# First feed-forward of a two-layer encoder: store issue, order of products, activation sums and conditioning work rearranged

## The chip, the cores and the metric

One core of a Trainium2 chip runs the whole program in one launch. The metric is the device time of that launch in microseconds (us), from three runs: a median of 2532.66, between 2530.72 and 2534.92.

## The reference

Input `x` is 1024 tokens by 1024 channels in float32; `c` is one conditioning vector of 1024. Two layers run one after the other. Each sub-layer computes `x <- LayerNorm(alpha*x + gate(c) * f(x*(1+scale(c)) + shift(c)))`.

```python
for l in range(2):
    sh1, sc1, g1, sh2, sc2, g2 = split(silu(c) @ w_ada[l] + b_ada[l], 6)
    h = x * (1 + sc1) + sh1
    if l == 0: y = short_conv_mixer(h)                  # W_out(B * conv3(C * V))
    else:      y = forgetting_attention(h, k, v, F)     # k, v, F from x after layer 0, own shift/scale
    x = layer_norm(alpha * x + g1 * y)
    h = x * (1 + sc2) + sh2
    y = (silu(h @ w_gate) * (h @ w_up)) @ w_down        # 1024 -> 2816 -> 1024
    x = layer_norm(alpha * x + g2 * y)
```

## The kernel before

The order of the work is: the convolution mixer of layer 0, the first feed-forward (layer 0), the shared K, V and forget gates with the queries (`kvq`), attention, and the second feed-forward. The activations lie channel-major: tile `x[k, half]` holds 128 channels by 512 tokens. Every matrix product in float32 is three matmuls (`mm3`, lines 169 to 171): each operand is split in a rounded part hi and a rest lo, and hi*hi, hi*lo and lo*hi are summed in PSUM. The split of a 128x1024 weight page is one ScalarE cast (line 655) and one VectorE subtraction (line 656) in `split_f`.

The first feed-forward is done by a Strassen-Winograd scheme: each matrix is cut in 2x2 blocks and seven block products M1 to M7 take the place of eight. `hidden` makes gate and up for 11 pairs of 128-channel tiles of the 2816 hidden channels; `down` then does the contraction. In `hidden` the work is a written list of **slots**, one product (j, n) each, pair j, n of M1 to M7. A slot is 24 matmuls of 128x512. There are 77: M1 and M2 of the six early pairs make the first 12, which are woven with the steps of the preceding LayerNorm for the second half of the tokens; then 65 slots run in a plain loop. An early pair has M5, M6, M3, M7 and, behind the next pair's first product, M4 there. A later pair has M1, M5, M6, M2, M3, M7 and its M4.

Each slot i does this in program order, and every engine keeps that order:

- `lq_pump(FRUN)`: issues loads from the written queue `lq` while more than FRUN pages are free. A page is 128x1024 float32; all loads, splits and results of this stage come from one first-in first-out list of free pages. The queue holds weight blocks (line 667, two DMAs for gate and up), the spilled M1 sums (815), stored blocks (822), and in each of the 65 slots one quarter of a conditioning group (755). All of them are issued on SP, the queue of SyncE.
- `ahead(i)`: the split of slot i+2, and on GpSimd the sums of weight blocks for slot i+3 (858 to 863, in place).
- the two halves of the product; behind each half its result leaves PSUM (`evac`): kept by ScalarE (895), summed with M1 on VectorE (900), or finished in `out` (913 silu input, 914 silu, 930 up part on VectorE, 931 product on GpSimd). `derive` (939, GpSimd) makes the sums of results that the contraction needs, and `store` (809) issues each to DRAM on SP as soon as it is written in the program. SP waits there until the data are ready.
- `ada_slot`: two VectorE multiply-adds (260, 262) on one quarter (two tiles of 128x512) of a conditioning group. A group is four quarters; when the next begins, four small TensorE transposes (295) and a VectorE reduction (297) finish it. What is left of the list is done in a loop behind the last slot.

The steps of the LayerNorm (`ln_steps`) are woven beside the 12 first slots. Each of the last four, `scale(k)` for k of 4 to 7, also runs the whole of `sums(k-4)` (lines 688 to 714): activation sums for M5, M6, M4, M7 and M3, two affine maps of x on GpSimd, and the store of two x tiles (738, SP).

`kvq` makes V (`values`) and K (`proj`) with 24 matmuls an item, and one `W.pump` now and then issues weights on SP.

Of the kernel before, what the change touches and what calls it, by code (L numbers as in the profile page):

```python
# [14 lines left out]
P = 128  # L15
# [62 lines left out]
class Builder:  # L78
# [369 lines left out]
    def ln_steps(self, half, tail, keep=False):  # L448
# [50 lines left out]
        return ([mean] + [lambda k=k: center(k) for k in range(KD)] + [var] + [lambda: None] * 2 + [spread]  # L499
                + [lambda k=k: scale(k) for k in range(KD)])  # L500
# [150 lines left out]
    def split_f(self, src, n=1024):  # L651

        nc = self.nc
        hi, lo = self.fpage((P, 1024), F32R), self.fpage((P, 1024), F32R)
        nc.scalar.copy(hi[:, 0:n], src)  # L655
        nc.vector.tensor_tensor(lo[:, 0:n], src, hi[:, 0:n], op=ALU.subtract)  # L656
        return hi, lo

# [13 lines left out]
    def sums_tail(self, vecs):  # L672
# [15 lines left out]
        def sums(k):  # L688
            K = k + 4
            a, a2 = A[:, k:k + 1], A[:, K:K + 1]  # L690
            z11, z12, z21, z22 = self.x[k, 0], self.x[k, 1], self.x[K, 0], self.x[K, 1]
            t = self.t("tmp", [P, HALF], tag="tA", bufs=3)
            u = self.t("tmp", [P, HALF], tag="tB", bufs=3)
            v = self.t("tmp", [P, HALF], tag="tA", bufs=3)
            w = self.t("tmp", [P, HALF], tag="tB", bufs=3)
            nc.gpsimd.tensor_scalar(t, z11, a, 1.0, op0=ALU.mult, op1=ALU.mult)
            nc.vector.scalar_tensor_tensor(u, z12, a, t, op0=ALU.mult, op1=ALU.subtract)
            put("M5", k, u, None, None)
            nc.vector.scalar_tensor_tensor(v, z22, a2, u, op0=ALU.mult, op1=ALU.subtract)
            put("M6", k, v, None, B[:, K:K + 1])  # L700
            nc.vector.scalar_tensor_tensor(w, z21, a2, v, op0=ALU.mult, op1=ALU.subtract)
            put("M4", k, w, None, None)
            nc.gpsimd.tensor_tensor(t, v, t, op=ALU.subtract)
            put("M7", k, t, None, BD[:, k:k + 1])
            h = self.T["M3"][k] = self.fpage((P, 2, HALF), F32R)
# [7 lines left out]
            self.x_out(k, K)  # L713
            self.sums_left -= 1

        def tail(k, half):
            if half == 0:
                n = "M1" if k < 4 else "M2"
                store = {}
                if (k, 0) in self.h:  # L720
                    self.drop("h", self.h.pop((k, 0)))
                self.modulate_tile(k, 0, self.x[k, 0], A, B, t_act=k % 2 == 0, lo_pool=k % 2 == 1, store=store)
                self.T[n][k % 4] = store[k, 0]
            elif k >= 4:
                sums(k - 4)
# [33 lines left out]
    def ada_slot(self):  # L759

        if not self.adal:
            return
        j, a = self.adal.pop(0)
        if a == 0:
            if self.adap:
                self.ada_finish(*self.adap)
            self.adap = None
            self.gacc = self.t("ada", [P, HALF], tag="ga", bufs=1)
        if a is None:
            return  # L770
        w = self.lq_get(("ada", j, a))
        for i in range(2):
            self.ada_step(self.gacc, w[:, i], 2 * a + i, self.nc.vector)
        self.lq_drop(("ada", j, a))
        if a == 3:
            self.adap = j, 4, self.gacc

    def hidden(self, l, nearly, left):
# [8 lines left out]
        nfirst = len(slots)  # L787
        late = None
        for j in range(npairs):
            names = ["M5", "M6", "M3", "M7"] if j in early else ["M1", "M5", "M6", "M2", "M3", "M7"]  # L790
# [16 lines left out]

        def store(n, j, t):
            nc.sync.dma_start(self.dr[n][j * P:(j + 1) * P], t)
            self.stored.add((n, j))  # L810
# [17 lines left out]
        def queue(lo, hi, ada):  # L828

            for i in range(lo, hi):  # L830
# [13 lines left out]
                if i >= nfirst and ada:  # L844
                    self.lq.append(ada.pop(0))
            self.lq += ada
# [18 lines left out]
        def parts(i):  # L865
# [3 lines left out]
            pre[i] = self.split_f(self.lq_get(key).rearrange("p m k c -> p (m k c)"))  # L869
            if e or n in end:  # L870
                self.lq_drop(key)

        def product(i, m):
# [13 lines left out]
            if m == 1:  # L887
                self.drop("f", *pre.pop(i))
# [13 lines left out]
        def leave(s, *names):  # L902
            for n in names:
                self.drop("f", s.pop(n))

        def out(j, r, half, s, m, bank, other):
# [16 lines left out]
            elif left and (r, half) == (0, 1):  # L923
                y = s["ya"][:, 1]
            else:
# [31 lines left out]
        def evac(i, m):  # L957
# [4 lines left out]
            if n == "M1":  # L962
                keep(s, "m1", m, X)
                if e and m:
                    nc.sync.dma_start(self.dr["m1"][j * P:(j + 1) * P], s["m1"].rearrange("p a b -> p (a b)"))
                    leave(s, "m1")
# [40 lines left out]
        def steps(i):  # L1007
            out = [lambda: ahead(i)]
# [4 lines left out]
            return out  # L1013
# [7 lines left out]
        def run(beside, before_end):  # L1021
            queue(2, len(slots), self.adaq_lq())
# [3 lines left out]
            for i in range(nfirst, len(slots)):  # L1026
                self.lq_pump(FRUN)
# [4 lines left out]
                self.ada_slot()  # L1032
            while self.adal:
                self.ada_slot()
            if self.adap:
                self.ada_finish(*self.adap)
                self.adap = None
        return begin, run

    def adaq_lq(self):  # L1040

        if self.adap:
            self.ada_finish(*self.adap)
            self.adap = None
        self.adal = [(j, a) for j in self.adaq for a in range(4)]
        self.adaq = []
# [50 lines left out]
    def down(self, update):  # L1097
# [37 lines left out]
        def part(ci, n, own, gi):  # L1135
# [7 lines left out]
            s = pg[:, 0:w].rearrange("p a b -> p (a b)")  # L1143
            if w == 2:
                pre[ci, n, own, gi] = self.split_f(s), None
            else:
                h = self.fpage((P, 2, HALF), F32R)
                nc.scalar.copy(h[:, 0], s)
                nc.vector.tensor_tensor(h[:, 1], s, h[:, 0], op=ALU.subtract)
                pre[ci, n, own, gi] = (h[:, 0], h[:, 1]), h  # L1150
            if not own or (key and n in ("M7", "M4", "M5", "M3")):
                self.lq_drop(key)
# [906 lines left out]
```

## Time and profile before

| | |
|---|---|
| median of 3 runs | 2532.66 us |
| profiled execution, its own time | 2534.88 us |
| its span (first to last instruction) | 2533.1 us |
| TensorE (PE) busy | 2396.6 us, 95% |
| VectorE (DVE) busy | 1508.8 us, 60% |
| GpSimd (POOL) busy | 854.6 us, 34% |
| ScalarE (ACT) busy | 825.4 us, 33% |
| mean granted TensorE clock | 0.98 |

All times in the rows count from the start of the span. A wait is listed as who waited for whom, with total us, number of times and longest. "SPq" is the queue of SyncE that issues DMAs. Matmul records can be missing by a few per cent, and the busy share of PE does not show how densely matmuls follow each other; their number in a stretch does.

### The profile page before, as it was taken

What the parts mean: (1) busy time and instruction counts of PE and PEld (TensorE: products, weight loads), DVE (VectorE), ACT (ScalarE), POOL (GpSimd) and SP (SyncE); (2) the same over time, 40 slices, a digit from 0 to 9 for tenths busy, and PEclk for the clock granted to TensorE, in tenths of its full rate; (3) what the DMA queues carried; (4) which work ended last, traced back from release to release, by engine and by line L of the source; (5) the groups of instructions that cost most, each with busy time, mean ns of one, the idle gap of its engine ahead of it and who ended that gap; (6) DMA issues with size and microseconds to landing.
All of it is one profiled execution on the core that took longest, in us unless ns stands there. A gap on an engine that the chain in (4) does not pass through costs nothing.

```text
span 2533.1 us, 29580 instructions
## 1 busy us (share of the span) xinstructions
PE 2396.6 (95%) x10905; PEld 1944.5 (77%) x10905; DVE 1508.8 (60%) x2129; ACT 825.4 (33%) x1321; POOL 854.6 (34%) x686
## 2 busy tenths in 40 slices
PE   7899999897899979999999999999999999999997
PEld 5688887676677868777877777777788888888886
DVE  5655558787768788887254567897632223232326
ACT  3311105421223323334233666666421111111113
POOL 6300003565555652325000556556330202030304
PEclk9999999998999989999999999998999999999999
DMA  8333204466655684412447566552211111111101
GB/s 267 122 98 118 86 26 131 150 201 208 200 174 191 225 327 137 150 34 100 151 144 237 166 182 155 143 136 72 64 42 50 50 50 50 48 44 50 46 30 67
DMA packets 286645, 311.95 MB, mean 123 GB/s; under 512 B 16068, under 2 KB 198548, under 8 KB 286500
## 3 DMA queue, kind: packets, MB, share of 16 engines
q1 hardware_dynamic: 274884, 284.69, 36.8%
q10 hardware_dynamic: 11616, 25.37, 2.7%
q8 instruction: 86, 1.41, 0.2%
q14 instruction: 59, 0.48, 0.1%
HBM read 252.91 MB, written 57.08 MB: 122 GB/s over the span
## 4 chain that ended last, share of the span: by engine, by line
PE 46%; DVE 4%; DMA 2%; ACT 2%; POOL 1%; issue 1%; SPq 0%; ACTq 0%; DVEq 0%; POOLq 0%
PE mm L169 13%; PE mm L171 13%; PE mm L170 12%; PE sm L1737 2%; PE s L1699 1%; PE mm L1749 1%; PE mm L1750 1%; PE s L1701 1%; DMA scr_ql<-tB 1%; DMA pg<-in_attn_w_q_dram 1%; DVE pg L1340 0%; ACT tA L1359 0%; DMA pg<-in_attn_w_o_dram 0%; POOL pg L161 0%; DVE pg L496 0%
## 5 line engine op out<-in xcount | busy, mean ns | idle before, releaser
L169 PE MATMUL mm<-pg,pg 128*128 128x512 f32 x3004 | 1189.8, 397 | 51.6 <-DVE pg L900 18.3
L170 PE MATMUL mm<-pg,pg 128*128 128x512 f32 x3004 | 1183.8, 394 | 11.5 <-DVE pg L370 6.6
L171 PE MATMUL mm<-pg,pg 128*128 128x512 f32 x3004 | 1183.3, 394 | 4.8 <-POOL pg L368 2.9
L169 PEld LDWEIGHTS mm<-pg,pg 128*128 128x128 f32 x3004 | 571.2, 190 | 179.3 <-DVE pg L900 16.0
L170 PEld LDWEIGHTS mm<-pg,pg 128*128 128x128 f32 x3004 | 571.5, 190 | 131.9 <-DVE pg L370 8.4
L171 PEld LDWEIGHTS mm<-pg,pg 128*128 128x128 f32 x3004 | 570.5, 190 | 127.8 <-POOL pg L368 3.8
L159 ACT CAST pg<-pg 128x1024 fp32r<-128x1024 f32 x144 | 150.5, 1053 | 591.7 <-PE mm L170 311.3
L656 DVE TENSOR_TENSOR pg<-pg,pg 128x1024 fp32r<-128x1024 f32 x147 | 220.0, 1507 | 78.5 <-ACT pg L655 62.1
L1338 POOL TENSOR_TENSOR pg<-pg,tB 128x512 f32<-128x512 f32 x80 | 107.6, 1346 | 463.0 <-DVE tB L1336 462.1
L163 DVE TENSOR_TENSOR pg<-pg,pg 128x1024 fp32r<-128x1024 f32 x124 | 154.3, 1248 | 171.1 <-ACT pg L159 168.7
L655 ACT CAST pg<-pg 128x1024 fp32r<-128x1024 f32 x147 | 151.1, 1048 | 284.0 <-POOL pg L939 55.1
L393 DVE TENSOR_TENSOR tB<-mm,tA 128x512 f32<-128x512 f32 x44 | 30.4, 692 | 216.4 <-PE mm L171 216.2
L1336 DVE TENSOR_TENSOR tB<-mm,pg 128x512 f32<-128x512 f32 x96 | 66.2, 690 | 134.7 <-PE mm L171 134.6
L262 DVE SCALAR_TENSOR_TENSOR ga<-pg,cact,ga 128x512 f32<-128x512 f32 x119 | 134.0, 1126 | 18.5 <-DMA pg<-in_w_ada_kv_dram 10.0
L1718 POOL TENSOR_SCALAR pg<-pg,st 128x512 f32<-128x512 f32 (+7 forms) x128 | 97.2, 767 | 122.4 <-DVE st L1716 115.4
L1741 DVE TENSOR_TENSOR pg<-sm,pg 128x512 fp32r<-128x512 f32 x192 | 104.1, 551 | 24.8 <-ACT pg L1740 22.2
L1740 ACT CAST pg<-sm 128x512 fp32r<-128x512 f32 x192 | 88.9, 479 | 49.1 <-PE sm L1737 45.5
L1715 ACT ACTIVATE pg<-s,st 128x512 f32<-128x512 f32 (+7 forms) x128 | 94.4, 743 | 28.6 <-DVE st L1712 19.1
L1709 DVE TENSOR_REDUCE st<-s 128x1 f32<-128x1024 f32 (+3 forms) x96 | 91.2, 951 | 15.2 <-PE s L1703 14.5
L1737 PE MATMUL sm<-ident,pg 128*128 128x128 f32 x576 | 97.9, 275 | 1.3 <-POOL pg L1718 1.0
L1118 POOL TENSOR_TENSOR pg<-pg,pg 128x1024 f32<-128x1024 f32 (+1 forms) x24 | 58.9, 2458 | 107.6 <-issue 40.8
L423 DVE SCALAR_TENSOR_TENSOR pg<-mm,mods,pg 128x512 f32<-128x512 f32 x96 | 70.7, 747 | 25.8 <-PE mm L171 25.2
(219 smaller groups left out, 2404.5 us busy)
## 6 DMA issues: line engine op xcount, KB each, us to landing
pg<-in_w_ada_dram SPq DMA_DIRECT2D x68, 512.0 KB
pg<-scr_hid SPq DMA_DIRECT2D x35, 512.0 KB
scr_hid<-pg SPq DMA_DIRECT2D x66, 256.0 KB
g<-in_w_ada_dram SPq DMA_DIRECT2D x56, 256.0 KB
pg<-in_ffn_w_gate_dram SPq DMA_DIRECT2D x56, 256.0 KB
pg<-in_ffn_w_up_dram SPq DMA_DIRECT2D x56, 256.0 KB
pg<-in_conv_w_in_dram SPq DMA_DIRECT2D x24, 512.0 KB
pg<-in_ffn_w_down_dram SPq DMA_DIRECT2D x44, 256.0 KB
```

The lines of the kernel that those rows point to most:

```text
L159: nc.scalar.copy(hi, raw)
L163: nc.vector.tensor_tensor(lo, raw, hi, op=ALU.subtract)
L169: mm(out, lhsT=whi, rhs=xhi, start=first, stop=False, skip_group_check=skip)
L170: mm(out, lhsT=whi, rhs=xlo, start=False, stop=False, skip_group_check=skip)
L171: mm(out, lhsT=wlo, rhs=xhi, start=False, stop=last, skip_group_check=skip)
L262: eng.scalar_tensor_tensor(acc, w, s, acc, op0=ALU.mult, op1=ALU.add)
L655: nc.scalar.copy(hi[:, 0:n], src)
L656: nc.vector.tensor_tensor(lo[:, 0:n], src, hi[:, 0:n], op=ALU.subtract)
L1338: nc.gpsimd.tensor_tensor(z, z, m, op=ALU.add)
L1718: nc.gpsimd.tensor_scalar(lg[:, i], lg[:, i], s[:, i:i + 1], 1.0, op0=ALU.mult, op1=ALU.mult)
L1737: nc.tensor.transpose(p[:, j * P:(j + 1) * P], lg[j][:, kt * P:(kt + 1) * P], self.c["ident"])
L1741: nc.vector.tensor_tensor(pt[:, 1, a:], p[:, a:], pt[:, 0, a:], op=ALU.subtract)
```

## The change

In `hidden`, a store is not issued where its data are made but noted with the number of its slot, and issued at the end of the next slot; pages that it reads go back to the free list with it. In an early pair the spill of M1 goes the same way. The last block of a pair, (1,0), is written over the one stored before it in page `yb` instead of into a small buffer. Later pairs go M1, M2, M5, M6, M3, M7. `sums(k)` becomes four steps, each a step of the weave, in the order 0, 4, 1, 5, 2, 6, 3, 7 of the scaled tiles, with two pages instead of small buffers; the x tiles are stored one k later. Conditioning quarters begin 16 slots later (ADA0), as many whole groups as fit in the slots that are left, and the others go beside `values` and `proj` in `kvq`, one quarter an item, through a single page. FRES goes from 9 to 11, FRUN from 7 to 5 (7 in the last 12 slots).

```diff
+        for k in tail.order if more else range(KD):
+            out += [lambda k=k: scale(k)] + (more(k) if more else [])
...
+    def later(self, age, fn):
+        self.pending.append((age, fn))
+    def flush(self, now=None):
+        while self.pending and (now is None or self.pending[0][0] < now):
+            self.pending.pop(0)[1]()
...
-        def sums(k):
+        def first(k):
+            a = A[:, k:k + 1]
+            box["pg"] = [self.fpage() for _ in range(2)]
+            t, u = box["t"], box["u"] = [pg[:, 0] for pg in box["pg"]]
+            nc.gpsimd.tensor_scalar(t, self.x[k, 0], a, 1.0, op0=ALU.mult, op1=ALU.mult)
+            nc.vector.scalar_tensor_tensor(u, self.x[k, 1], a, t, op0=ALU.mult, op1=ALU.subtract)
+            put("M5", k, u, None, None)
+            if k:
+                self.x_out(k - 1, k + 3)
+
+        def second(k):
...
+            put("M6", k, v, None, B[:, K:K + 1])
...
+        def third(k):
...
+            put("M4", k, w, None, None)
             nc.gpsimd.tensor_tensor(t, v, t, op=ALU.subtract)
             put("M7", k, t, None, BD[:, k:k + 1])
...
+        def fourth(k):
...
+        tail.order = (0, 4, 1, 5, 2, 6, 3, 7)
+        tail.more = lambda k: [lambda f=f: f(k - 4) for f in (first, second, third, fourth)] if k >= 4 else []
...
+    def ada_item(self):
+        nc = self.nc
+        if self.adan:
+            j, a, w = self.adan
+            self.adan = None
+            if a == 0:
+                self.ada_end()
+                self.gacc = self.t("ada", [P, HALF], tag="ga", bufs=1)
+            self.ada_quarter(j, a, w)
+            self.drop("att", w)
+        elif not self.adaq:
+            self.ada_end()
+        if self.adaq and self.pages["att"]:
+            j, a = self.adaq[0], self.adaa
+            w = self.page("att", (P, 2, HALF), F32)
+            nc.sync.dma_start(w, self.ada_cols(j, 4).rearrange("(k p) c -> p k c", p=P)[:, 2 * a:2 * a + 2])
...
-            names = ["M5", "M6", "M3", "M7"] if j in early else ["M1", "M5", "M6", "M2", "M3", "M7"]
+            names = ["M5", "M6", "M3", "M7"] if j in early else ["M1", "M2", "M5", "M6", "M3", "M7"]
...
         def store(n, j, t):
-            nc.sync.dma_start(self.dr[n][j * P:(j + 1) * P], t)
-            self.stored.add((n, j))
+            def fn():
+                nc.sync.dma_start(self.dr[n][j * P:(j + 1) * P], t)
+                self.stored.add((n, j))
+            self.later(self.slot, fn)
...
+            elif (r, half) == (1, 0):
+                self.flush(self.slot)
+                y = s["yb"][:, 0]
...
+            return out + [lambda: self.flush(i)]
...
-                self.lq_pump(FRUN)
+                self.lq_pump(FRUN if i < len(slots) - 12 else FRUN + 2)
...
-                self.ada_slot()
-            while self.adal:
-                self.ada_slot()
+                if i >= nada:
+                    self.ada_slot()
...
-FRES = 9
-FRUN = 7
+FRES = 11
+FRUN = 5
+ADA0 = 16
```

In `down`, a chunk with a single pair now takes two pages for its hi and lo instead of one, and the reserve is counted accordingly.

## Rows read from the trace of the kernel before

**Rows 1.** The page, part 1: busy us, share of the span, instructions.
```profile
PE 2396.6 (95%) x10905; PEld 1944.5 (77%) x10905; DVE 1508.8 (60%) x2129; ACT 825.4 (33%) x1321; POOL 854.6 (34%) x686
```

**Rows 2.** Busy time of each engine by stage; granted clock, DMA share, GB/s last.
```profile
405.00:500.50 95.50, 83.85 (x360) 66.54 (x361) 80.03 (x97) 47.76 (x70) 50.14 (x30) 0.98 0.41 138
500.50:605.00 104.50, 91.36 (x374) 73.35 (x375) 87.14 (x85) 21.25 (x25) 64.50 (x32) 0.92 0.63 202
605.00:693.00 88.00, 70.88 (x297) 56.96 (x297) 60.87 (x73) 17.56 (x20) 48.66 (x26) 0.92 0.62 199
693.00:760.00 67.00, 61.37 (x266) 49.37 (x267) 45.86 (x50) 17.71 (x25) 36.90 (x19) 0.97 0.56 178
760.00:917.50 157.50, 150.95 (x665) 123.87 (x664) 124.38 (x126) 51.63 (x70) 85.97 (x43) 0.98 0.70 236
917.50:957.00 39.50, 31.03 (x129) 25.03 (x128) 39.09 (x34) 11.42 (x12) 20.64 (x9) 0.87 0.75 278
...
1200.00:1400.00 200.00, 196.80 (x877) 159.48 (x876) 84.66 (x128) 66.17 (x98) 5.58 (x11) 1.00 0.55 175
1900.00:1950.00 50.00, 50.00 (x223) 41.39 (x222) 11.48 (x13) 10.36 (x14) 0.00 (x0) 1.00 0.17 51
```

**Rows 3.** Waits of PE in 500.5 to 917.5: total us, times, longest.
```profile
PE mm L169 <- DVE pg L900: 18.3, 5, 7.4
PE sm L295 <- DVE ga L262: 10.4, 2, 7.4
```

**Rows 4.** Waits of SP, the DMA issuing queue, in 500.5 to 917.5.
```profile
SPq L809 <- POOL pg L939: 115.6, 42, 11.5
SPq L809 <- POOL pg L931: 65.3, 12, 13.0
SPq L809 <- POOL tB L931: 43.4, 6, 9.4
SPq L667 <- DVE pg L656: 12.6, 4, 3.8
```

**Rows 5.** Waits of POOL in 500.5 to 917.5.
```profile
POOL pg L858 <- DMA pg<-in_ffn_w_up_dram: 71.9, 7, 13.7
```

**Rows 6.** Timeline of SP from 600.9 to 626: start, us, what, count.
```profile
600.94 0.37 SPq L755 DMA_DIRECT2D pg<-in_w_ada_kv_dram  x1
604.29 4.26 SPq L809 DMA_DIRECT2D scr_hid<-pg  x3
...
609.14 0.43 SPq L667 DMA_DIRECT2D pg<-in_ffn_w_gate_dram  x1
609.62 0.51 SPq L667 DMA_DIRECT2D pg<-in_ffn_w_up_dram  x1
```

**Rows 7.** Timeline of POOL in the same stretch; idle time before it in brackets.
```profile
615.13 2.39 POOL L858 TENSOR_TENSOR pg<-pg,pg 128x1024 f32<-128x1024 f32 x1 [6.92 <-DMA pg<-in_ffn_w_gate_dram]
```

**Rows 8.** Timeline of DVE in the same stretch.
```profile
623.62 1.22 DVE L656 TENSOR_TENSOR pg<-pg,pg 128x1024 fp32r<-128x1024 f32 x1 [11.33 <-ACT pg L655]
```

**Rows 9.** Timeline of PE in the same stretch.
```profile
625.50 0.80 PE L169 MATMUL mm<-pg,pg 128*128 128x512 f32 x1 [7.36 <-DVE pg L900]
```

**Rows 10.** Line 755, the loads of conditioning quarters: ns min/median/max, first and last start.
```profile
L755 SPq DMA_DIRECT2D pg<-in_w_ada_dram x52: 367/390/1477, 491.8 to 889.0; - x52
L755 SPq DMA_DIRECT2D pg<-in_w_ada_kv_dram x16: 368/386/1947, 523.7 to 626.1; - x16
```

**Rows 11.** DVE by line in 500.5 to 605: busy, mean ns, idle before.
```profile
L262 DVE SCALAR_TENSOR_TENSOR ga<-pg,cact,ga 128x512 f32<-128x512 f32 x26 | 31.8, 1223 | 10.1 <-DMA pg<-in_w_ada_kv_dram 10.0
```

**Rows 12.** Waits of PE in 405 to 500.5.
```profile
PE mm L169 <- ACT pg L895: 5.8, 3, 4.4
PE mm L169 <- ACT pg L682: 3.1, 1, 3.1
```

**Rows 13.** Waits of PE in 917.5 to 960.
```profile
PE sm L295 <- DVE ga L262: 8.1, 1, 8.1
```

**Rows 14.** Waits of DVE in 500.5 to 917.5.
```profile
DVE pg L656 <- DMA scr_hid<-pg: 10.9, 3, 7.9
```

More of the change, by code (lines that the diff above doesn't have):

```diff
@@ L498, in scale @@
                 tail(k, half)
-        return ([mean] + [lambda k=k: center(k) for k in range(KD)] + [var] + [lambda: None] * 2 + [spread]
-                + [lambda k=k: scale(k) for k in range(KD)])
+        more = getattr(tail, "more", None) if half else None
+        out = [mean] + [lambda k=k: center(k) for k in range(KD)] + [var] + [lambda: None] * 2 + [spread]
+        for k in tail.order if more else range(KD):
+            out += [lambda k=k: scale(k)] + (more(k) if more else [])
+        return out
     def vec(self):
@@ L868, in parts @@
             key = ("e" if e else "", j, *src[n])
-            pre[i] = self.split_f(self.lq_get(key).rearrange("p m k c -> p (m k c)"))
-            if e or n in end:
-                self.lq_drop(key)
+            ends = e or n in end
+            pre[i] = self.split_f(self.lq_get(key), last=ends)
+            if ends:
+                self.blk.pop(key)
         def product(i, m):
@@ L1007, in steps, with begin @@
         def steps(i):
-            out = [lambda: ahead(i)]
+            def begin():
+                self.slot = i
+                ahead(i)
+            out = [begin]
             if i < nfirst:
@@ L1021, in run @@
         def run(beside, before_end):
-            queue(2, len(slots), self.adaq_lq())
+            queue(2, len(slots), self.adaq_lq((len(slots) - nada) // 4))
             self.down_queue()
@@ L1142, in part @@
             pg = self.lq_get(key) if key else E[ci, gi]
[L1143 to L1152, printed above, removed]
+            ends = not own or n in ("M7", "M4", "M5", "M3")
+            pre[ci, n, own, gi] = self.split_f(pg, w * HALF, ends)
+            if ends:
+                self.blk.pop(key)
         def prepare(pi):
@@ L1175, in forget @@
                 for own in (True, False):
-                    pair, h = pre.pop((ci, n, own, gi))
-                    self.drop("f", *([h] if h is not None else pair))
+                    self.drop("f", *pre.pop((ci, n, own, gi)))
         for f in prepare(0):
@@ L1215, in down @@
                     left_steps.pop(0)()
-                held = sum(1 if h is not None else 2 for _, h in pre.values())
-                self.lq_pump(FDOWN - held - len(E))
+                self.lq_pump(FDOWN - 2 * len(pre))
                 yield ci, n, o
@@ L1597, in kvq @@
                 proj("k", f, half, 1.0, "kh", "kl")
+                self.ada_item()
             W.done(("k", f))
```

101 lines of the change are left out of this document (59 added, 42 removed).

## The prediction

> **What bounds the kernel now.** I read four views, in this order. The page says that PE is busy for 95% of the span [rows 1], so the first impression is that only fewer matmuls would help, and the change removes none. The windows by stage correct that. In a stretch where nothing stalls, 223 matmuls start in 50 us, as in the last row of [rows 2]; I take 222, so 0.225 us each, and call the time of a stage above its number of matmuls times 0.225 its loss. The conditioning transposes, some 64 of them in the middle of it, are counted at the same price. By the counts of [rows 2]:
>
> - 405 to 500.5 (first 12 slots beside the LayerNorm): 360 matmuls are worth 81.1, loss 14.4
> - 500.5 to 605: 374, 84.2, loss 20.3
> - 605 to 693: 297, 66.9, loss 21.1
> - 693 to 917.5: 266 + 665 = 931, 209.7, loss 14.8
> - 917.5 to 957 (last slot done, contraction begins): 129, 29.1, loss 10.4
>
> Together 81 us. Records are missing: the 65 slots and 16 groups that the program has in 500.5 to 917.5 make 1560 + 64 = 1624 matmuls and the rows count 1602, so 5 us of it is no loss. In K and V, 1200 to 1400, 877 are worth 197.5, loss 2.5: nothing can be won there and something can be lost.
>
> Third, who waits for whom. In 500.5 to 917.5 PE waits for VectorE's sums of results (18.3 us) and for the conditioning accumulator before its transposes (10.4) [rows 3]. Part of the loss is in no wait: the granted clock is 0.92 from 500.5 to 693 and 0.87 behind 917.5, against 1.00 in K and V [rows 2]. At a mean of 0.92 about 0.16 of the time is at the lower level, 1.2 instead of 2.4 GHz, which comes with the stalls.
>
> Fourth, why VectorE is late. SP stands for 224 us (115.6 + 65.3 + 43.4, 60 waits) of the 417 at a store whose data GpSimd has not written yet [rows 4], and GpSimd's weight sums wait 71.9 us for weights [rows 5], which SP issues behind those stores. One case shows the ring. Three stores go out from 604.29, the last at about 608.2; only then the next pair's weights are issued, from 609.14 [rows 6]. GpSimd has been idle 6.92 us when it can add them, at 615.13 [rows 7]. VectorE, which has the split of a later product ahead of the sum of this one in its order, is idle 11.33 us, starts the split at 623.62 [rows 8] and the sum behind it, and PE, which waits for that sum, starts at 625.50, after 7.36 us of nothing [rows 9]. So the stage is bound by a ring of in-order queues: store waits for GpSimd, weights for the store, GpSimd for the weights, split, result, PE.
>
> **The change part by part.**
>
> *Stores one product later, two more pages for loads.* The loads pumped in slot i+1 now stand ahead of the stores of slot i. In the case above the weights could go as soon as SP is free of its load of 600.94, at about 601.3 [rows 6], 8 us sooner, more than the 7.36 of the stall. What is late next is the page: the loads themselves wait only 12.6 us for pages in this stage [rows 4], but the free list gets shorter, because pages under a store come back one slot later; the two pages of FRUN give that back. In 605 to 693 I take 12 of the 21.1 (bounds 0 and 20): VectorE has 60.9 us of work there [rows 2] for 66.9 us of matmuls, so a split that is a little late still shows. In 693 to 917.5, where pairs are longer and the loss is small, I take 6 of 14.8, the earlier M2 included, which frees its two banks and gives its weight sums a slot more (bounds 0 and 12).
>
> *No conditioning in the first 16 of the 65 slots.* These 16 are worth 86.5 us and lie in 500.5 to about 610. Of the 68 quarters [rows 10] 48 stay, one a slot, so 20, five groups, leave the stage. VectorE has 87.1 us of work in 500.5 to 605, of which 31.8 are the multiply-adds [rows 2, 11]; without them some 50 us are left, and it is no bound any more. Both waits for the accumulator, 10.4 [rows 3], lie in this window and go. The deferred stores act here too. I take 15 of 20.3; bounds 10 (the two waits alone) and 20.
>
> *Conditioning behind the last slot.* Before, 65 of 68 quarters fit the slots and three come behind, with the last transposes stalling PE for 8.1 us [rows 13] while VectorE is busy 39.09 of 39.5 us [rows 2]. After, 48 quarters and a closing step fit the last 49 slots. I take 8 of 10.4; bounds 0 and 10.
>
> *Small steps of the sums.* PE waits 8.9 us in this stage for results that ScalarE copies behind the lump of a sum [rows 12]. The work is the same and VectorE has 80 of 95.5 us, more than the 81.1 of matmuls leave free, so not all of it goes. The LayerNorm's own steps are pressed into an earlier, shorter part of the weave, which can cost. I take 5; bounds a loss of 5, if those earlier steps collect the waits instead, and a gain of 9.
>
> *Conditioning beside K and V.* The 20 quarters need no new matmuls: their 20 transposes come with them. VectorE is busy 84.7 of 200 us there, GpSimd 5.6, DMA at 0.55 [rows 2], so 40 multiply-adds of 1.2 us [rows 11] fit in its idle time. The new waits are VectorE's for the quarter's load (behind it in the queue stand the results of K and V, which six banks cover for some products), SP's for the one page (behind it stand weight loads), and PE's for the accumulator, five times. Nothing of this is in the trace of before in this stage; the nearest row is a PE wait of 7.4 [rows 3], so the bounds are 0 and 5 x 7.4 = 37. Here the accumulator is done a whole product before PE asks for it and VectorE is half idle, so I take 1.
>
> *Writing (1,0) over the stored block.* VectorE's write in M4 now waits until the store of M7, two slots earlier, has been read out. It is issued at the end of the slot between, so about one product, 24 x 0.225 = 5.4 us, is left for it. The nearest row is VectorE waiting for a store 3 times, 10.9 us together, 7.9 at most [rows 14]. Bounds 0 and 11 pairs x 7.9 = 87; as only three of all the stores were waited for, I take 0 and keep the upper end for a rival.
> The Trainium skill (DMA: Bandwidth & Descriptors, Anatomy of one DMA) fits a transfer, on another issuing path, as about 2.0 us plus bytes over 436 GB/s; for a store of 256 KB that is an estimate of 2.6 us, under one product, and by it this wait would not exist. The row's 7.9 us says that it can.
>
> Page counts in the contraction change by nothing that is near the path: 0.
>
> *Sum.* 5 + 15 + 12 + 6 + 8 - 1 = 45 us. The profiled execution took 2534.9, so 2489.9; it stood 2.2 above the median of the runs, so 2488. Adding the good ends, 9 + 20 + 20 + 12 + 10 = 71, gives 2462; the bad ends of all but the overwrite, 10 - 5 - 37 = -32, give 2565.
>
> **The rivals.**
>
> *Pages, not stores, set the loads* (faster, but less). If loads are issued on demand because no page is free, taking stores out of SP's way moves them little; the pages held one slot longer then eat what FRUN gives. For it: SP also waits for pages where it loads weights. Against: 12.6 us of that against 224 at stores [rows 4]. Only the conditioning's terms stay: 10 + 8 = 18, so 2533 - 18 = 2515.
>
> *The overwrite becomes the wait* (slower). Place: VectorE's second half of M4, 11 times. If SP comes late to the store, because loads that wait for pages now stand ahead of it, VectorE stands, and with it the next splits. Price: 3.6 us each (10.9 / 3) plus the delayed store of M4 and page behind it, together up to 7.9, so 40 to 87 us, while the terms of the deferral, 12 + 6, go. 45 - 18 = 27 are won elsewhere; at 7.9 the balance is 60 lost, at 3.6 it is 13 lost: 2546, up to 2593. It decides from 27 / 11 = 2.5 us a pair on. For it: SP's longest wait is 13.0 [rows 4]. Against: M7's block is ready early in the slot between.
>
> *K and V pay it back.* One accumulator late five times, 37 us: 2488 + 36 = 2524. For it: weight loads and quarters share SP's order and one page. Against: VectorE is idle for more than half of the stage.
>
> **How the numbers follow.** The forecast, with its own range of 2462 to 2508, has a chance of 0.63; less by pages, 2515, 0.16; K and V, 2524, 0.08; slower by the overwrite 0.11; 0.02 for a stage that gains everything. A measurement of this kernel can tell about 0.2%, 5 us, from no change. Faster by more than that: 0.63 + 0.16 + 0.02 and most of the K and V case, with a little off for mixtures of two rivals, 0.82; within it 0.06; slower 0.12. The range from 2458 to 2532 takes in the two faster rivals and leaves out the slower one, some of the no-change cases and the far low end.
>
> **What would show it.** Right: SP's waits at line 809 fall well below 224 us and weights are issued before the stores of the slot before; GpSimd's 71.9 us for weights shrink; 500.5 to 605 becomes some 15 us shorter, with the clock back near 1.00; no 8 us hole behind the last slot; K and V within 2 us of before. Wrong: VectorE waiting for `scr_hid` in line 930 or 928 (overwrite); SP waiting for pages at line 667 (pages); PE waiting at line 295 behind 1200 (K and V). If 605 to 693 keeps its loss although SP no longer waits at stores, VectorE's own work was the bound and the ring was not.

## The result, and the profile after

The changed kernel takes 2518.05 us (median of 4 runs, 2514.95 to 2518.77); beside it on the same chip the kernel before took 2531.9. The ratio is 0.9941, interval 0.9924 to 0.9958: faster by 14 us. The profiled executions, 2534.88 before and 2518.77 after, differ by 16.1, where 45 were forecast; 2518 lies inside the range.

Where the 16 us come from is read from the same events in both traces (us from the span's start; a slot by its result on VectorE, V by ScalarE's copy of its first result; the last slot, M4, is left out, because after the change its result stands behind work of the contraction):

| event | before | after | gain so far | forecast so far |
|---|---|---|---|---|
| 3rd of the 65 slots | 517.9 | 513.5 | 4.3 | 5 |
| 14th slot | 600.2 | 572.5 | 27.8 | 20 |
| 28th slot | 696.1 | 674.8 | 21.3 | 32 |
| 64th slot (M7 of the last pair) | 910.1 | 882.9 | 27.2 | 38 |
| first LayerNorm mean behind the contraction | 1126.9 | 1094.4 | 32.5 | 46 |
| first result of V | 1163.6 | 1130.5 | 33.2 | 46 |
| first attention score | 1384.5 | 1368.7 | 15.8 | 45 |
| end of the span | 2533.1 | 2517.0 | 16.1 | 45 |

The feed-forward won 33 us, and the stretch from the first V result to the first score gave 17 of them back. The page and the stages, against [rows 1] and [rows 2]:

```profile
PE 2400.4 (95%) x10905; PEld 1948.8 (77%) x10905; DVE 1497.8 (60%) x2129; ACT 827.3 (33%) x1321; POOL 860.0 (34%) x686
```

```profile
405.00:500.00 95.00, 83.78 (x352) 65.91 (x353) 89.00 (x105) 49.82 (x74) 53.07 (x31) 0.96 0.48 160
500.00:605.00 105.00, 102.90 (x447) 84.66 (x447) 51.72 (x55) 23.37 (x27) 69.23 (x35) 0.98 0.54 170
605.00:693.00 88.00, 75.09 (x304) 60.76 (x303) 69.52 (x67) 19.09 (x23) 53.40 (x27) 0.90 0.53 171
693.00:760.00 67.00, 63.67 (x280) 52.24 (x279) 54.97 (x58) 20.93 (x29) 38.20 (x19) 0.97 0.67 216
760.00:900.00 140.00, 136.90 (x607) 112.52 (x606) 114.63 (x113) 47.79 (x63) 82.13 (x41) 0.99 0.70 244
1130.00:1200.00 70.00, 68.33 (x299) 55.41 (x298) 44.45 (x63) 28.26 (x41) 20.14 (x17) 0.98 0.61 197
1200.00:1325.00 125.00, 115.17 (x501) 91.72 (x500) 69.27 (x111) 38.84 (x52) 2.40 (x4) 0.96 0.59 188
```

With the forecast's 0.225 us a matmul the loss from 405 to 500 stayed, 95 - 352 x 0.225 = 15.8 for 14.4; from 500 to 605 it fell from 20.3 to 105 - 447 x 0.225 = 4.4; from 605 to 693 it stayed, 19.6 for 21.1, at a granted clock of 0.90; in K and V it rose from 2.5 to 195 - 800 x 0.225 = 15.0. PE's busy share of 95% is the same and tells none of this.

The waits from 500 to 900, by SP, POOL, PE and DVE (engine, tile, line, releaser: us, times, longest). Line 868 is the store, 681 the weight load, 783 the quarter's load, 260 and 262 the multiply-adds, 660 the split, 962 and 999 results with M1 and the up part, 918 and 921 weight sums:

```profile
SPq L868 <- POOL pg L1008: 102.2, 41, 11.9
SPq L868 <- POOL pg L1000: 73.4, 17, 9.1
...
POOL pg L918 <- DMA pg<-in_ffn_w_up_dram: 49.8, 8, 11.5
POOL pg L921 <- DMA pg<-in_ffn_w_up_dram: 20.6, 5, 8.1
...
PE mm L169 <- DVE tA L979: 11.4, 3, 6.0
PE mm L169 <- DVE pg L962: 5.1, 2, 3.0
PE sm L295 <- DVE ga L262: 4.1, 2, 3.9
...
DVE ga L262 <- DMA pg<-in_w_ada_kv_dram: 11.8, 2, 7.8
DVE ga L260 <- DMA pg<-in_w_ada_dram: 8.0, 1, 8.0
DVE pg L660 <- DMA scr_hid<-pg: 6.2, 1, 6.2
DVE ga L262 <- DMA pg<-in_w_ada_dram: 6.1, 1, 6.1
DVE pg L999 <- DMA scr_hid<-pg: 5.4, 2, 2.7
```

SP still stands 176 us at stores for GpSimd, for 224 in [rows 4]. GpSimd's wait for weights fell from 71.9 [rows 5] to 49.8 at the same line, and with the second line from 96.9 to 70.4. VectorE waits 25.9 us for quarters that have not landed. It did so before too, for 16.9 us; but now all 25.9 lie in the 14 slots from the 14th to the 28th, where it was 3.3. The waits before, by POOL and DVE from 500 to 917, then by DVE and PE in those 14 slots:

```profile
POOL pg L861 <- DMA pg<-in_ffn_w_up_dram: 25.0, 4, 7.4
...
DVE ga L262 <- DMA pg<-in_w_ada_kv_dram: 10.0, 3, 5.1
DVE ga L262 <- DMA pg<-in_w_ada_dram: 6.9, 4, 3.1
```

```profile
DVE ga L262 <- DMA pg<-in_w_ada_dram: 3.3, 2, 2.6
...
PE mm L169 <- DVE pg L900: 15.8, 3, 7.4
```

PE's wait for the sums with M1 there, the end of the forecast's ring, went from 15.8 to 5.1 (line 962 above); 6.0 at line 979 and 3.9 at the accumulator came in its place. One case after the change, DVE first, then PE:

```profile
592.88 0.49 DVE L260 TENSOR_SCALAR ga<-pg,cact 128x512 f32<-128x512 f32 x1 [7.97 <-DMA pg<-in_w_ada_dram]
...
603.32 0.75 DVE L262 SCALAR_TENSOR_TENSOR ga<-pg,cact,ga 128x512 f32<-128x512 f32 x1 [6.06 <-DMA pg<-in_w_ada_dram]
...
607.42 2.80 DVE L660 TENSOR_TENSOR pg<-pg,pg 128x1024 fp32r<-128x1024 f32 x1
610.15 3.42 DVE L262 SCALAR_TENSOR_TENSOR ga<-pg,cact,ga 128x512 f32<-128x512 f32 x2
```

```profile
614.32 0.77 PE L169 MATMUL mm<-pg,pg 128*128 128x512 f32 x1 [6.04 <-DVE tA L979]
```

VectorE idles 8 and 6 us at a quarter, then does the multiply-adds and the split that piled up behind it, and PE pays 6 us later for a result that stands behind those.

In K and V VectorE stands at 12 of the 20 quarters. DVE beside V (line 1576 is the V result), then the issue of one quarter:

```profile
1199.92 0.74 DVE L262 SCALAR_TENSOR_TENSOR ga<-pg,cact,ga 128x512 f32<-128x512 f32 x1
1204.82 0.75 DVE L262 SCALAR_TENSOR_TENSOR ga<-pg,cact,ga 128x512 f32<-128x512 f32 x1 [4.16 <-DMA pg<-in_w_ada_dram]
1205.49 0.68 DVE L1576 TENSOR_TENSOR pg<-mm,pg 128x512 fp32r<-128x512 f32 x1
1206.09 0.74 DVE L262 SCALAR_TENSOR_TENSOR ga<-pg,cact,ga 128x512 f32<-128x512 f32 x1
1211.17 0.75 DVE L262 SCALAR_TENSOR_TENSOR ga<-pg,cact,ga 128x512 f32<-128x512 f32 x1 [4.34 <-DMA pg<-in_w_ada_dram]
```

```profile
1206.87 0.37 SPq L827 DMA_DIRECT2D pg<-in_w_ada_dram  x1
```

The next quarter can be asked for only when its one page is free, at the end of the second multiply-add; it lands some 4 us later; and VectorE, which keeps its order, does not take the V result behind it earlier. The loop has a period of 1211.17 - 1204.82 = 6.35 us, where the product has 5.4. But PE waits for none of these V results: the banks between them hold. The waits of DVE and PE from 1130 to 1325:

```profile
DVE ga L262 <- DMA pg<-in_w_ada_dram: 34.3, 10, 4.5
DVE ga L260 <- DMA pg<-in_w_ada_dram: 4.5, 2, 2.4
...
PE sm L1642 <- DVE pg L1636: 5.0, 1, 5.0
PE sm L295 <- DVE ga L262: 4.8, 3, 2.2
```

Lines 1636 and 1642 are the forget gates' scan on VectorE and the transposes that wait for it; line 295 are the transposes that finish a conditioning group. What PE does beside V, then at the last V product's end and at the gates:

```profile
1165.00:1200.00 35.00, 35.00 (x158) 28.92 (x156) 15.17 (x21) 10.00 (x14) 0.59 (x2) 1.00 0.66 212
1225.00:1245.00 20.00, 17.80 (x74) 12.81 (x73) 9.10 (x17) 5.92 (x9) 0.00 (x0) 0.91 0.67 217
1245.00:1270.00 25.00, 19.98 (x83) 15.37 (x82) 18.80 (x30) 13.59 (x16) 0.00 (x0) 0.86 0.51 157
```

```profile
1237.89 0.80 PE L295 MATMUL sm<-ident,ga 128*128 128x128 f32 x4 [2.20 <-DVE ga L262]
...
1238.92 0.63 PE L1619 MATMUL mm<-pg,tB 128*64 128x512 f32 x1
1239.34 0.63 PE L1618 MATMUL mm<-pg,tB 128*64 128x512 f32 x1
```

Beside V the products run at full pace, 158 matmuls in 35 us. From the first V result to the first score the 17.3 us more are: 4.8 at the accumulator, 4.2 more at the gates' transposes (5.0 for 0.8 before), and some 4.8 in 22 matmuls that start 0.43 us apart instead of 0.225, at the lower clock, behind these waits and one in the LayerNorm. The rest, 3.5, is not split further; the run without loads below, which has the same transposes and multiply-adds, is 2.5 longer than before.

### The profile page after: what moved, and what is told of

Its sections match the earlier page's. It is cut to its first block, busy times and chain, and to the rows that moved or that the text cites. A ratio compares the mean times of both kernels' runs of the same rounds, so it can differ in the third digit from the quotient of the medians.

```text
span 2517.0 us, 29595 instructions
## 1 busy us (share of the span) xinstructions
PE 2400.4 (95%) x10905; PEld 1948.8 (77%) x10905; DVE 1497.8 (60%) x2129; ACT 827.3 (33%) x1321; POOL 860.0 (34%) x686
## 5 line engine op out<-in xcount | busy, mean ns | idle before, releaser
L169 PE MATMUL mm<-pg,pg 128*128 128x512 f32 x3004 | 1188.8, 397 | 35.8 <-DVE tA L979 11.4
L170 PE MATMUL mm<-pg,pg 128*128 128x512 f32 x3004 | 1186.1, 395 | 14.5 <-DVE pg L370 7.2
L171 PE MATMUL mm<-pg,pg 128*128 128x512 f32 x3004 | 1183.8, 394 | 3.6 <-POOL pg L368 2.6
L159 ACT CAST pg<-pg 128x1024 fp32r<-128x1024 f32 x144 | 150.5, 1052 | 586.2 <-PE mm L170 301.1
L660 DVE TENSOR_TENSOR pg<-pg,pg 128x1024 fp32r<-128x1024 f32 (+1 forms) x161 | 245.5, 1535 | 59.0 <-ACT pg L659 34.3
L659 ACT CAST pg<-pg 128x1024 fp32r<-128x1024 f32 (+1 forms) x161 | 159.7, 1013 | 285.6 <-DVE pg L660 81.6
L163 DVE TENSOR_TENSOR pg<-pg,pg 128x1024 fp32r<-128x1024 f32 x124 | 154.2, 1248 | 151.9 <-ACT pg L159 149.4
L262 DVE SCALAR_TENSOR_TENSOR ga<-pg,cact,ga 128x512 f32<-128x512 f32 x119 | 115.0, 966 | 53.9 <-DMA pg<-in_w_ada_dram 40.3
L1819 PE MATMUL mm<-pg,pg 128*128 128x512 f32 x192 | 80.3, 418 | 5.9 <-ACT pg L1810 4.7
```

The source lines that it names most:

```text
L159: nc.scalar.copy(hi, raw)
L163: nc.vector.tensor_tensor(lo, raw, hi, op=ALU.subtract)
L169: mm(out, lhsT=whi, rhs=xhi, start=first, stop=False, skip_group_check=skip)
L170: mm(out, lhsT=whi, rhs=xlo, start=False, stop=False, skip_group_check=skip)
L171: mm(out, lhsT=wlo, rhs=xhi, start=False, stop=last, skip_group_check=skip)
L262: eng.scalar_tensor_tensor(acc, w, s, acc, op0=ALU.mult, op1=ALU.add)
```

## The experiments

Each ratio is against the kernel before, run on the same chip; the changed kernel's is 0.9941. "V to attention" is the time from the first V result to the first attention score: 220.9 before, 238.2 after. "Slots" is the gain at the 64th slot (after 27.2), "14 slots" the time from the 14th to the 28th slot (before 95.9, after 102.3).

### The conditioning beside K and V

Left out, the five groups' columns set to zero:

```diff
-        self.adaq, self.adan, self.adaa = self.adaq[n:], None, 0
+        for j in self.adaq[n:]:
+            self.nc.gpsimd.memset(self.mods[:, j:j + 4], 0.0)
+        self.adaq, self.adan, self.adaa = [], None, 0
```

> The changed kernel without the five conditioning groups beside K and V (they are left out, their vectors are zero, so the layer-1 outputs are not the reference's). Between the profiles the feed-forward won 33 us and the stretch from the first V product to the first attention score gave 17 back. If the quarters cause that: about 2501, the stretch from V to attention 221 us long as before, against 238 now. If something else of the change does (weights arriving later, the moved close of the pool): 2518 and 238.

Measured 0.9894 (0.9878 to 0.9909). V to attention 222.8, slots 28.5. So the payback is this conditioning's, and its place is right: without it the granted clock is 1.00 in both windows, against 0.98 and 0.96 above:

```profile
1130.00:1200.00 70.00, 68.65 (x304) 55.55 (x303) 39.68 (x52) 29.41 (x42) 20.07 (x19) 1.00 0.50 169
1200.00:1325.00 125.00, 122.20 (x543) 98.76 (x542) 58.10 (x88) 43.81 (x58) 1.45 (x3) 1.00 0.47 152
```

Two half loads into a page that is kept, so that the first half is asked for while the second is still in use:

```diff
-            nc.sync.dma_start(w, self.ada_cols(j, 4).rearrange("(k p) c -> p k c", p=P)[:, 2 * a:2 * a + 2])
+            for i in range(2):
+                nc.sync.dma_start(w[:, i], self.ada_cols(j, 4)[(2 * a + i) * P:(2 * a + i + 1) * P])
...
```

> The changed kernel; beside K and V each quarter is loaded as two halves of 256 KB into the same page, each half as soon as its own multiply-add is done. Theory: one page makes a loop of multiply-add, issue, 4 us of load, multiply-add, with the result of V or K between, 6.2 us an item against 5.4 us of matmuls; then about 2503 and V to attention within 4 us of before (221). Rival: the extra DMA traffic or the VectorE work itself delays the stage; then 2518, V to attention 238, as in the changed kernel.

0.9914 (0.9897 to 0.9930), V to attention 232.3: a third of the payback is gone, less than the "within 4 us of before" that was expected. PE's wait for the accumulator falls from 4.8 to 1.0.

### Work or load

All loads kept, but the multiply-adds of three quarters in four left out (here and in the slots):

```diff
-        for i in range(2):
+        for i in range(2 if a == 0 else 0):
```

> The changed kernel with all quarters loaded as changed, but VectorE's multiply-adds done for the first quarter of each group alone (three quarters of the conditioning sums from the feed-forward on are left out). Theory: VectorE, in order, stands at a multiply-add until its quarter has landed, and the results of the products stand behind it. Then the 14 slots from M7 of the third pair to M3 of the sixth, 102 us in the changed kernel, 77 at full pace, take under 88, and V to attention is within 5 of 221. Rival: the loads themselves (SP's order, pages, DMA) are the cost; then 98 to 104 us, and 233 to 240.

All multiply-adds kept, on data that is there already, and no loads:

```diff
-            self.nc.sync.dma_start(w, self.ada_cols(j, 4).rearrange("(k p) c -> p k c", p=P)[:, 2 * a:2 * a + 2])
-            return w
+            return self.fpage((P, 2, HALF))
...
```

> The changed kernel without the loads of the quarters in the feed-forward and beside K and V; the multiply-adds are all done, on data that lie there (the conditioning vectors are wrong). A page is still taken for each. Theory of the wait: the 14 slots take under 88 us as in the kernel without multiply-adds and V to attention 221 to 226. Rival, VectorE's own work is the bound: still 98 to 104, and above 232.

Without most of the work 0.9827 (0.9808 to 0.9847), 14 slots 90.2, V to attention 225.3; without the loads 0.9908 (0.9889 to 0.9928), 87.0 and 223.4. Either alone removes most of the payback beside K and V and brings the 14 slots under those of before; PE's wait for the accumulator beside K and V is gone in both. The same window of three kernels, the changed one, then without loads, then without most of the work:

```profile
595.00:690.00 95.00, 81.59 (x324) 65.96 (x325) 70.47 (x71) 19.20 (x22) 53.81 (x27) 0.89 0.58 188
```

```profile
595.00:690.00 95.00, 86.34 (x375) 70.63 (x374) 70.85 (x71) 22.88 (x27) 60.14 (x31) 0.96 0.36 115
```

```profile
595.00:690.00 95.00, 83.82 (x365) 67.71 (x366) 46.87 (x57) 20.77 (x25) 58.51 (x31) 0.98 0.65 208
```

VectorE does the same work in the second, 70.85 us for 70.47, and PE starts 51 matmuls more; in the third more bytes move, 208 GB/s for 188, and PE starts 41 more. So neither VectorE's work alone nor the transfer alone is the bound; what both runs take away is that VectorE must stand still until a transfer has landed. (Without loads SP and the pages are relieved too, and in all 65 slots that kernel won 25.9 us, no more than the changed one; the later pairs gave it back, which was not followed further.)

Asked for one slot earlier in the slots, halves beside K and V, and no quarter behind the last three V products and the first K products:

```diff
+        if self.adal:
+            j, a = self.adal.pop(0)
+            self.adah = j, a, self.lq_get(("ada", j, a))
...
-                self.ada_item()
+                if half == 0 or t == 0:
+                    self.ada_item()
...
-                self.ada_item()
+                if f > 2:
+                    self.ada_item()
...
```

> The changed kernel with three things: in the feed-forward each quarter is asked for one slot before its multiply-adds; beside K and V it is loaded in halves; and there no quarter is worked on behind the last three V products and the first K pair, where VectorE has the chain of the forget gates. Theory of the wait: a load takes about 4.5 us and a slot 5.4, so the waits go: the 14 slots 102 to about 90, V to attention 232 with halves alone to about 225; in all some 2535 - 15 - 13 - 12 = 2495 where before is 2535. Rival, pages: one page more is held, other loads come later, the 14 slots stay at 102 or above; then some 2507.

0.9971 (0.9959 to 0.9982); 14 slots 102.4, V to attention 238.7, of which some 8 is a stall of its own between the last K product and the first query. The 90 and the 225 that were expected did not come. One slot is not ahead enough: from 572 to 675 VectorE still waits 20.3 us for quarters, at most 7.8 at a time.

So no run shows that asking earlier cures these slots. What the traces do show is that in the kernels with the change the length of these slots goes roughly with this wait (the last three are described below; the other runs, but for the one with nothing deferred, have 25 to 27 and 102 to 104):

| | VectorE's waits for quarters in the 14 slots | 14 slots |
|---|---|---|
| changed | 25.9 | 102.3 |
| asked one slot earlier | 20.3 | 102.4 |
| without most of the work | 8.1 | 90.2 |
| without loads | 0 | 87.0 |
| conditioning as before | 14.9 | 98.0 |
| reserve of 7 pages | 14.0 | 96.4 |
| more at the convolution | 2.9 | 85.7 |

At full pace they would take 14 x 24 x 0.225 = 75.6 and a few transposes, so some 10 us are there without any quarter. The kernel before, 3.3 and 95.9, does not belong in the table: it has the 15.8 us at the sums. Nor does the one with nothing deferred, 15.4 and 101.3: its VectorE waits 16.3 more for stores.

### Other places for that work

Seven groups more beside the convolution mixer at the launch's start, ten in the last 41 slots, none beside K and V:

```diff
-            self.adaw = 2
+            self.adaw = 1
-ADA0 = 16
+ADA0 = 24
...
```

> The changed kernel with 14 conditioning groups instead of 7 done in the convolution, where VectorE was busy 26 to 34 of 50 us, the other 10 in the last 41 slots of the feed-forward, none beside K and V. Theory of the wait: the slots up to the sixth pair run at nearly full pace (14 slots under 85 us), K and V take 221; the convolution, whose products have six banks to wait in, pays nothing: 2535 - 15 - 17 - 17 = 2486. Rival: VectorE's waits for loads show in the convolution in place of the feed-forward: 7 groups of about 4 us, and 2510 or more.

0.9904 (0.9880 to 0.9929). V to attention is 221.0, as before, and the convolution is 20 us longer, where VectorE now waits 49.5 us for such loads between 20 and 400 (22.1 in the changed kernel). The 14 slots, most of which have no quarter now, take 85.7. On GpSimd instead of VectorE, in halves, and with a group's transposes one item later:

```diff
-            self.ada_quarter(j, a, w)
+            self.ada_quarter(j, a, w, nc.gpsimd)
...
```

> The changed kernel with the quarters beside K and V worked on by GpSimd, which has 5 of 200 us of work there, instead of VectorE; loaded in halves, and each group's transposes one item later. Theory of the wait: what is late is then behind nobody, so V to attention takes 221 to 226 instead of 238, and the whole 2535 - 15 - 14 = 2506 where before is 2535. Rival: the 10 MB of loads take the weights of K and Q their share of DMA: then still 232 or more and about 2516.

0.9968 (0.9958 to 0.9979), V to attention 236.7, where 221 to 226 was expected: there is no wait for the accumulator any more, but one for what GpSimd owes PE, a LayerNorm step (368), and the gates' chain stays late. Waits of PE from 1133 to 1375:

```profile
PE sm L1649 <- DVE pg L1643: 6.4, 1, 6.4
PE mm L171 <- POOL pg L368: 4.9, 1, 4.9
```

### The deferral and the first 16 slots

Stores and the return of pages at once, as before:

```diff
-        self.pending.append((age, fn))
+        fn()
```

> The changed kernel with every store issued and its pages returned where the data are made, as before; all else as changed. Forecast's theory (weights were late because SP stood at stores): the middle of the stage loses again, 15 to 25 us, so about 2536, SP's waits at stores above 210 us. Rival (the deferral moved nothing that decides; the early slots got faster because conditioning left them): 2518 within 5 us.

All 17 groups in the slots from the first on, as before, nothing beside K and V:

```diff
-            queue(2, len(slots), self.adaq_lq((len(slots) - nada) // 4))
+            queue(2, len(slots), self.adaq_lq(len(self.adaq)))
-ADA0 = 16
+ADA0 = 0
...
```

> The changed kernel with all 17 conditioning groups in the feed-forward from the first of the 65 slots, the rest behind the last slot, none beside K and V, as before; stores deferred, small steps, order and reserves as changed. If the missing conditioning made the first 16 of the slots faster: these lose 17 us again and the end about 6, K and V wins 17: 2518 + 23 - 17 = 2524. If the deferred stores did: the 33 us of the feed-forward stay but for the 6 at its end, and K and V wins 17: about 2507.

Stores issued at once, but the spill's page still back one slot later:

```diff
-            def fn():
-                nc.sync.dma_start(self.dr[n][j * P:(j + 1) * P], t)
-                self.stored.add((n, j))
-            self.later(self.slot, fn)
+            nc.sync.dma_start(self.dr[n][j * P:(j + 1) * P], t)
+            self.stored.add((n, j))
...
+                    self.later(i, lambda t=t: self.drop("f", t))
```

> The changed kernel with each store issued at once, as before, but the pages under stores given back one slot later, as changed. With stores and pages both at once the changed kernel was 17 us slower, SP's waits at stores the same 184 us in both, and VectorE waited 27 us for stores to be read out. Theory: the later return of the pages is what the deferral brings, so this run equals the changed kernel within 5 us (ratio 0.994). Rival, the forecast's: loads pass the stores on SP; then this is 12 to 17 us slower than the changed kernel (ratio 1.000).

| | ratio | gain at 14th slot | 14 slots | slots |
|---|---|---|---|---|
| changed | 0.9941 (0.9924 to 0.9958) | 27.8 | 102.3 | 27.2 |
| nothing deferred | 1.0008 (0.9998 to 1.0019) | 13.6 | 101.3 | 13.7 |
| conditioning as before | 0.9978 (0.9969 to 0.9987) | 6.0 | 98.0 | 10.7 |
| only pages deferred | 0.9952 (0.9936 to 0.9968) | 27.9 | 103.7 | 25.3 |

The deferral is worth 0.67%, and all of it is won before the 14th slot. But the order of stores and loads on SP has no part in it that can be seen: with stores at once it is kept, if only the page comes back later; and SP stands at stores for GpSimd 183 us with nothing deferred and 176 in the changed kernel, where "above 210" was expected. The view that shows why is VectorE's waits for stores to be read out, 500 to 905, with nothing deferred:

```profile
DVE pg L962 <- DMA scr_hid<-pg: 37.0, 6, 12.6
DVE pg L999 <- DMA scr_hid<-pg: 9.9, 4, 4.7
DVE pg L660 <- DMA scr_hid<-pg: 6.2, 1, 6.2
```

That is 53.1 us, 13.7 in the changed kernel (lines 660, 997 and 999 for it), and with only pages deferred the one row is

```profile
DVE pg L997 <- DMA scr_hid<-pg: 5.2, 2, 2.7
```

The free list is first in, first out and short. A page handed back while its store has only been issued, and waits for GpSimd on SP, is soon the next one out, and a result of VectorE then waits for that store. In [rows 14], before the rest of the change, this was 10.9; so the deferral mends, at least in part, what the rest of the change had brought, and what it would be worth in the kernel before was not tried. Conditioning as before was slower than either of its two forecasts, 2524 and 2507: what is left of it behind the last slot costs too. From the 64th slot to the LayerNorm mean that kernel loses 4.3 us to the one before (10.7, then 6.4), where the changed one wins 5.3.

### Order of products and reserve

```diff
-            names = [...] if j in early else ["M1", "M2", "M5", "M6", "M3", "M7"]
+            names = [...] if j in early else ["M1", "M5", "M6", "M2", "M3", "M7"]
```

> The changed kernel with later pairs in the old order M1, M5, M6, M2, M3, M7. The forecast had the order within the 6 us of 693 to 917.5. If it brings something it is in the five later pairs alone: from the last product of the sixth pair to the end of the slots, 3 to 6 us longer; rival, nothing: within 2 us.

```diff
-                self.lq_pump(FRUN if i < len(slots) - 12 else FRUN + 2)
+                self.lq_pump(7)
```

> The changed kernel with the old reserve of 7 pages all through. The forecast said that FRUN 5 gives back what the later return of pages takes. If loads are held up by pages: the slots get slower, 5 to 15 us, with GpSimd waiting more for weights than 88 us in the slots; if not, within 3 us.

The old order: 0.9927 (0.9907 to 0.9947), slots 32.5, so the earlier M2 costs some 5 us in the trace; the ratios' intervals overlap. A reserve of 7 all through: 0.9966 (0.9954 to 0.9978), slots 26.3. Inside the slots it moves a loss: the gain at the 14th is 23.0 for 27.8, and the 14 slots take 96.4 for 102.3, as before the change. SP stands at the quarters' loads for the last users of their pages 54.3 us in the changed kernel, 24.2 here and 19.7 before. So the smaller reserve is one reason why quarters come late.

### Both remedies together

Old order, half loads, and no quarter behind the last three V products and the first K product:

```diff
-                self.ada_item()
+                if half == 0 or t == 0:
+                    self.ada_item()
...
-                self.ada_item()
+                if f > 2 or half:
+                    self.ada_item()
...
```

> The changed kernel with the old order in later pairs, quarters loaded in halves beside K and V, and none worked on behind the last three V products and the first K product, where VectorE has the chain of the forget gates. Theory: VectorE's waits at quarters are what K and V lose, and with the halves the rest of it (232 against 221 us from V to attention) lies in that chain; then 222 to 228, the five later pairs 5 us shorter than in the changed kernel, in all 0.986 to 0.989 of before. Rival: what is left with halves comes from the load traffic, wherever the work stands; then 232 still and 0.990 to 0.991.

0.9876 (0.9855 to 0.9897), median 2502.9: faster than both kernels, and it leaves nothing out. Slots 31.6, V to attention 228.6. Of VectorE's waits for quarters from 1130 to 1325 this is left, in halves; PE waits 0.4 at the accumulator and 3.1 at the gates' transposes, and 5 matmuls are slow instead of 22:

```profile
DVE ga L262 <- DMA pg<-in_w_ada_dram: 23.1, 18, 3.1
```

In parts, from first to last V result, from there to the gates' transposes, and on to the first score:

| | V | gates | K to attention |
|---|---|---|---|
| before | 101.2 | 15.4 | 104.4 |
| changed | 108.1 | 22.6 | 107.5 |
| no quarters there | 101.1 | 17.3 | 104.3 |
| halves | 104.6 | 20.2 | 107.4 |
| both remedies | 104.6 | 17.7 | 106.4 |

Without any quarter the gates take 17.3, so the 17.7 with both remedies is about all that can be had there: halves won 2.4 and the new place of the quarters 2.5. What V and K still lose, 3.5 and 2, goes with the waits that are left; no run parts it further.

## Why the prediction was wrong

**The term that was mis-sized: "Conditioning beside K and V", taken at 1, measured 17.** Its upper end was 37, and the rival "K and V pay it back" gave 2524. The forecast counted VectorE's idle time (84.7 busy of 200) and found room for 40 multiply-adds. Room it had: most of them even ran faster than counted, 0.77 us each for 1.2. And "six banks cover" the wait held: PE waited for no result of V or K. What failed is the sentence that "the accumulator is done a whole product before PE asks for it". A share of idle time says nothing of an engine that keeps its order and must stand at an operand on its way: that time is idle and closed. With a loop of 6.35 for a product of 5.4 VectorE falls behind, and PE meets that where it needs VectorE at once: three times at the accumulator, 4.8 us, which is the rival's mechanism at a smaller size, and 4.2 more at the gates' transposes, a place that no part of the prediction names. The slower matmuls, some 4.8, were in no sum either.

**The step that failed: "Stores one product later", 12 in 605 to 693.** These slots lost 6.4 us. SP stood at stores for 176 us, so the test that the prediction set itself, "well below 224", was met only in part. The deferral does win 13.5 us of the slots, but earlier, and by pages that come back later. The ring of the case in [rows 6 to 9] was read rightly as a case; and its stall at the sums did shrink in the 14 slots, from 15.8 to 5.1; but that nothing else would take its place was concluded from SP's 224 us, which is time in which a queue waits, not time that anyone lacks. In its place VectorE waits 25.9 us there for quarters. The prediction's other reading, "If 605 to 693 keeps its loss ... VectorE's own work was the bound", is wrong as well: its premise on SP held only in part, and with all that work and no loads the loss from 605 to 693 fell from 19.6 to 88 - 346 x 0.225 = 10.2. The 6 us of 693 to 917.5 came out as 5.9, but with nothing deferred it is 5.5, so not by the reason given.

**Right.** The first 16 slots: clock 0.98 instead of 0.92 and a loss of 4.4. Conditioning as before takes 16.5 us off the slots' gain (forecast 15); but at the 14th slot it takes 21.8 of 27.8, and doing without the deferral 14.2, so the two do not simply add. The tail: 5.3 us from the 64th slot to the LayerNorm (forecast 8), the 8 us hole of [rows 13] gone. Three runs that are the same up to there won 2.6 to 4.3, and with the conditioning as before the same stretch loses 4.3.

**Right by luck.** The first part won 4.3 by the third slot, for 5 forecast. But PE's waits for ScalarE's results in the first 12 slots, which the small steps were to cut, are 8.6 for 8.9, and with the conditioning in the slots as before the gain at the third slot is gone (-0.4). So the small steps are not shown to win anything:

```profile
PE mm L169 <- ACT pg L957: 8.6, 4, 3.6
```

**The rivals.** The overwrite as a wait, the slower rival, did not come: VectorE waits 7.5 us at lines 997 and 999 for stores. "Pages, not stores, set the loads", 2515, came nearest in time, and pages did matter: by results that took one too soon, and by quarters whose loads had to wait for one.

**Open.** What it takes to have the quarters of the slots from the 17th on there in time: one slot earlier did not do it; a larger reserve halves the wait but loses as much elsewhere, and nothing with more pages in all was tried.

## What to carry to other kernels

Work put into an engine's idle time is free only if its operands are there: give it as many pages as it takes to ask for the next one a whole item ahead, and compare the loop (issue, landing, use, page free) with the item that it runs beside. Buffers of results hide a lag only until somebody needs the lagging engine at once, so look for that place first. A page under a store that still waits for its data should not go back to a first-in first-out list that is short. A queue's waiting time ranks nothing; take away the wait and see whether the stage moves.

## What the hardware showed

- A quarter of 512 KB needs 4.1 to 4.3 us from issue to use beside V: issued at 1200.69 and 1206.87 (line 827), used at 1204.82 and 1211.17. The Trainium skill (DMA: Bandwidth & Descriptors, Anatomy of one DMA) would give 2.0 us plus bytes over 436 GB/s, an estimate of 3.2 us, for another issuing path; the measurement decides. By that estimate the loop would be 5.4 us, no longer than the product.
- The same multiply-add took 771 ns on average from 1130 to 1325, where GpSimd is busy 22.5 of 195 us, and 1048 ns from 500 to 900, where it is busy 243 of 400; before, 1223 [rows 11].
- Where TensorE waited for VectorE, the granted clock is lower: 0.90 from 605 to 693, 0.86 from 1245 to 1270, 1.00 in K and V without the quarters. Behind its waits of 2.2 and 5.0 us beside V and at the gates, matmuls start 0.43 us apart, the lower of its two levels (1.2 and 2.4 GHz), instead of 0.225.
